# Half-tile weight buffers, a longer lead for the casts, and a third seven-product group per feed-forward block

## The chip, the cores and the metric

The kernel runs on one core of a Trainium2 chip. The metric is the device time of one execution in microseconds (us). The engines named below are PE (TensorE; PEld is its weight load), DVE (VectorE), ACT (ScalarE), POOL (GpSimd) and SP (SyncE, whose queue issues most DMAs). Each engine takes its instructions in order.

## What is computed

A trunk of two layers over 256 tokens of width 1024, float32. Cut to what matters here:

```python
D_MODEL, SEQ, DEPTH, D_FF = 1024, 256, 2, 2816

def swiglu(h, w_gate, w_up, w_down):
    return (jax.nn.silu(h @ w_gate) * (h @ w_up)) @ w_down

for l in range(DEPTH):
    x = x + 0.5 * swiglu(rms_norm(x, ffn1_norm[l]), ffn1_w_gate[l], ffn1_w_up[l], ffn1_w_down[l])
    ...            # one projection, windowed and differential attention, output projection
    x = x + 0.5 * swiglu(rms_norm(x, ffn2_norm[l]), ffn2_w_gate[l], ffn2_w_up[l], ffn2_w_down[l])
return rms_norm(x, final_norm)
```

So there are four feed-forward blocks (FFNs), two in a layer, with an attention stage ("mix") between the two of a layer. Every weight is read from HBM once or more and used on 256 tokens.

## The kernel before

**Precision.** A float32 matrix product is made of three fast ones. Each operand is split into a rounded part (`hi`, by a cast on ACT) and the rest (`lo`, by a subtraction on DVE); the product is hi·hi + lo·hi + hi·lo. Weights are split on the way in: `emit_split` (L167) casts a weight tile in pieces, each piece one ACT cast and one DVE subtraction of 128 x 1024 elements (128 x 512 for tiles in the set `fine`). So a weight tile costs ACT and DVE time as well as PE time.

**Weight tiles and their queue.** A weight tile is 512 rows by 512 columns (1 MB, held as 128 x 4 x 512), or as much in another shape. `specs` lists all tiles of the program in the order in which PE uses them. Three counters run ahead of the use: `dma` (the load, by SP, into one of N_RAW = 6 buffers `raw`), `prep` (what must be done to the raw tile first) and `split`. `weights()` (L219) hands out the next tile and first calls `ahead()` (L198), which issues whatever is due: splits up to LOOK = 2 tiles ahead of the one in use, preps one further, loads up to AHEAD = 8 tiles ahead while a raw buffer is free. The split parts lie in three whole-tile buffers `whi` and three `wlo`. In the feed-forward blocks the order in which instructions are issued is kept on every engine, so a split that is issued before a subtraction of results also runs before it.

**An FFN.** The 2816 hidden columns are taken in five groups of 512 (0 to 4) and a rest of 256. For a group, the hidden activations of 256 tokens are made from the gate and up weights; the next group's work contains the "down" product of this group's hidden values (two tiles, 24 matmuls each, L632). For it the hidden block is turned: eight PE transposes, then an ACT cast and a DVE subtraction for each of two blocks (`turn`, L618, and `split`, L485; the result is the tile `s` in the profile, called hT here). A plain group takes eight products of 12 matmuls: two token halves, two halves of the contraction, gate and up.

**By seven.** The groups in SEVEN = (2, 4) take seven products instead (Strassen's scheme, over token halves by contraction halves by gate/up; `by_seven`, L579). The sums of the token side are made once in an FFN (`make_sums`, during group 1). The sums on the weight side are made for each group by `seven` (L115) from four quarters: a (gate, upper rows), b (up, upper rows), c (up, lower rows), d (gate, lower rows). The nine steps of a seven group, in the order of use:

| step | weights | product | how the raw tile is made |
|---|---|---|---|
| 1 | a | p1 | load |
| 2 | b + c | p7 | load b, then POOL issues an accumulating DMA of c onto it (the "c-gather") |
| 3 | a + b + c | p6 | DVE adds a onto b's buffer (two adds); then POOL adds b from HBM onto a's buffer (the "b-gather") |
| 4 | down, first half | | load |
| 5 | d | p2 | load |
| 6 | a + b + c + d | p4 | DVE adds b's buffer onto d's (two adds); b's buffer is then free |
| 7 | a + b | p5 | a's buffer, after the b-gather |
| 8 | c | p3 | load |
| 9 | down, second half | | load |

hT is turned between p7 and p6; the combinations of products (u2, u3, g0, g1) are DVE instructions on 128 x 512 elements, the two `up` are the last step of the hidden values.

Loads go out on SP in the order of steps, each when a raw buffer comes free. Both gathers read 1 MB from HBM again, on POOL's DMA queue. The c-gather is issued behind its own load (`behind`, L164), the b-gather behind the two adds of step 3.

The diff touches, besides these, `tokens`, `narrow` and `prod` (which part of a tile a matmul reads), the calls of `weights` in `ffn`, `ffn_end`, `ffn_close`, `mix` and `out_part`, and the buffers of the token sums (L320).

Of the kernel before, what the change touches and what calls it, by code (L numbers as in the profile page):

```python
# [10 lines left out]
F32R = mybir.dt.float32r  # L11
AF = mybir.ActivationFunctionType
ALU = mybir.AluOpType
# [11 lines left out]
QA, KA, VA, QB, KB, VB = 0, 512, 640, 768, 1280, 1792  # L25
BIG = 1e33

LOOK, AHEAD = 2, 8
N_RAW, N_HI, N_LO = 6, 3, 3
N_S4 = 16  # L30
SEVEN = (2, 4)


@with_exitstack
def trunk(ctx: ExitStack, tc: tile.TileContext, x, n1, g1, u1, d1, nm, w_in, sink,
# [128 lines left out]
        if s.behind is not None:  # L164
            s.behind()

    def emit_split(i):  # L167
        s = specs[i]
        kn, n, raw = s.kn, s.n, raws[s.src]
        hi = wp.tile([P, kn, n], F32R, tag="whi", bufs=N_HI, name=nm_("whi"))  # L170
        lo = wp.tile([P, kn, n], F32R, tag="wlo", bufs=N_LO, name=nm_("wlo"))
        loaded[i] = (hi, lo)
        cuts = [0, kn // 2, kn] if i > 1 and (i not in fine or kn < 4) else [kn * j // 4 for j in range(5)]
        for a, b in zip(cuts, cuts[1:]):
            if n == D:
                views = [(t[0][:, a:b, c:c + 512], t[1][:, a:b, c:c + 512], t[2][:, a:b, c:c + 512])
                         for t in [(raw, hi, lo)] for c in (0, 512)]
            elif i not in paired:
                views = [(raw[:, a:b], hi[:, a:b], lo[:, a:b])]
            else:  # L180
                views = [(raw.rearrange("p k (s c d) -> p c k s d", s=2, c=2)[:, c, a:b],
                          hi.rearrange("p k (c s d) -> p c k s d", s=2, c=2)[:, c, a:b],
                          lo.rearrange("p k (c s d) -> p c k s d", s=2, c=2)[:, c, a:b]) for c in range(2)]
            for r_, h_, l_ in views:
                act.copy(h_, r_)
                dve.tensor_tensor(l_, r_, f(h_), op=ALU.subtract)
            if i < 2:
                yield
        for k in s.free:
            raws.pop(k)  # L190

    def emit_early(i):
        yield from emit_dma(i)
        yield from emit_split(i)

    at = dict(use=0, dma=2, prep=2, split=2)

    def ahead(n):  # L198

        n = min(n, len(specs) - 1)  # L200
        while True:
            if at["split"] <= n and at["prep"] > at["split"]:
                for _ in emit_split(at["split"]):
                    pass
                at["split"] += 1
            elif at["prep"] <= min(n + 1, len(specs) - 1) and at["dma"] > at["prep"] and \
                    (specs[at["prep"]].prep is None or at["split"] >= at["prep"]):
                if specs[at["prep"]].prep is not None:
                    specs[at["prep"]].prep()
                at["prep"] += 1  # L210
            elif at["dma"] < min(at["use"] + AHEAD, len(specs)) and (specs[at["dma"]].moves is None or len(raws) < N_RAW):
                if specs[at["dma"]].moves is not None:
                    for _ in emit_dma(at["dma"]):
                        pass
                at["dma"] += 1
            else:
                break

    def weights(look=LOOK):  # L219
        i = at["use"]  # L220
        at["use"] += 1
        if i > 1:
            ahead(i + look)
        return loaded.pop(i)

    for l in range(DEPTH):
        def ffn_specs(wg, wu, wd):
# [45 lines left out]
    class Norm:  # L273
# [30 lines left out]
        def make_sums(self):  # L304

            self.sm = []

            def part(b, t):

                vs = [f(self.xs[2 * b + i]) for i in range(2)]  # L310
                return [[v[:, :, c + t * P:c + (t + 1) * P] for v in vs] for c in (0, S)]

            def make(x, y, op, rest):
                v = tmp().rearrange("p a (c s) -> p (a c) s", c=2)
                for i in range(2):
                    vi = v[:, 2 * i:2 * i + 2]
                    dve.tensor_tensor(vi, x[i], y[i], op=op)
                    for z, o in rest:
                        dve.tensor_tensor(vi, vi, z[i], op=o)
                sm = blk().rearrange("p a (c s) -> p (a c) s", c=2)  # L320
                act.copy(sm[:, :, 0:P], v)
                dve.tensor_tensor(sm[:, :, P:S], v, f(sm[:, :, 0:P]), op=ALU.subtract)
                self.sm.append(sm)
                return [v[:, 0:2], v[:, 2:4]]

            add, sub = ALU.add, ALU.subtract
            (t0h, t0l), (t1h, t1l), (b0h, b0l), (b1h, b1l) = [part(b, t) for b in range(2) for t in range(2)]
            s1 = make(b1h, t1h, sub, [(b1l, add), (t1l, sub)])
            yield
            s2 = make(s1, t0h, add, [(t0l, add)])  # L330
            yield
            make(t1h, t0h, sub, [(t1l, add), (t0l, sub)])
            yield
            make(b0h, s2, sub, [(b0l, add)])
            yield
# [53 lines left out]
    def take_x(k):  # L389
# [8 lines left out]
        elif k == 1:  # L398
            for e in (g, u, g, u):
                next(e)  # L400
            norm.pair(2)
            ahead(2)
            norm.pair(3)
        elif k == 2:
            ahead(3)
            for t in range(2):
                for h in range(2):
                    norm.squares(t, h * 512, 512)
            norm.stats()
            constants()  # L410
# [60 lines left out]
            dve.tensor_scalar_mul(gsub[:, l:l + 1], gcol[:, 48 + l:49 + l], 1.0 - lam_init[l])  # L471


    def tokens(accs, xs, w, k0, ks=range(4), first=0, last=KC - 1, order=None):

        hi, lo = w
        for k, t in (order or [(k, t) for k in ks for t in range(2)]):
            kk = k0 + k
            xv = xs[kk // 2][:, kk % 2]
            xh, xl = xv[:, t * P:(t + 1) * P], xv[:, S + t * P:S + (t + 1) * P]  # L480
            pe.matmul(accs[t], lhsT=xh, rhs=hi[:, k], start=kk == first, stop=False)
            pe.matmul(accs[t], lhsT=xl, rhs=hi[:, k], start=False, stop=False)
            pe.matmul(accs[t], lhsT=xh, rhs=lo[:, k], start=False, stop=kk == (last if isinstance(last, int) else last[t]))

    def split(dst, src, scale=None):  # L485

# [7 lines left out]

    def narrow(acc, w, j, xs, kcs, first, last):

        hi, lo = w
        for i, (wk, xk) in enumerate(kcs):
            wh = hi[:, wk, j * P:(j + 1) * P]
            wl = lo[:, wk, j * P:(j + 1) * P]  # L500
            xv = xs[xk // 2][:, xk % 2]
            pe.matmul(acc, lhsT=wh, rhs=xv[:, 0:S], start=first and i == 0 and j == 0, stop=False)
            pe.matmul(acc, lhsT=wh, rhs=xv[:, S:512], start=False, stop=False)
# [43 lines left out]
    def ffn(norm, aside=None, before=None, final=False):  # L547
# [19 lines left out]
            return h  # L567

        def prod(xo, w):
            hi, lo = w  # L570
            acc = bank()
            for k in range(4):
                xh, xl = xo(k)
                pe.matmul(acc, lhsT=xh, rhs=hi[:, k], start=k == 0, stop=False)
                pe.matmul(acc, lhsT=xl, rhs=hi[:, k], start=False, stop=False)
                pe.matmul(acc, lhsT=xh, rhs=lo[:, k], start=False, stop=k == 3)
            return acc

        def by_seven(h, g):  # L579
# [8 lines left out]
            p1 = prod(norm.quarter(0, 0), weights())  # L588
            m1 = flat()
            act.copy(m1, p1)  # L590
            p7 = prod(norm.summed(2), weights())
            hT = turn(h, 2)
            p6 = prod(norm.summed(1), weights())
            u2 = put(flat(), p6, m1, ALU.subtract)
# [42 lines left out]
        if before is None:  # L637
            before = norm.late
        before(0)
        ws = (weights(), weights(LOOK - 1))  # L640
        for k in (0, 2):
            if k:
                before(1)
# [40 lines left out]
    def ffn_end(parts, last):  # L684
# [4 lines left out]
        w = {0: weights()}  # L689

        def group(h, order, a=None, c=slice(None), first=0):
            tokens(a or accs[h], hT, [t[:, :, c] for t in w[h]], G4, first=first, last=last[h], order=order)

        def tail(h, order=BY_TOKENS, a=None, c=slice(None)):
            tokens(a or accs[h], [None] * (2 * NGRP) + hE, [t[:, h, :, c] for t in w["rest"]], 4 * NGRP, last=last[h], order=order)

        group(0, [(k, t) for k in range(3) for t in range(2)])
        hE.extend(rest())
        group(0, [(3, t) for t in range(2)])
        w["rest"] = [t.rearrange("p k (h n) -> p h k n", h=2) for t in weights()]  # L700
        w[1] = weights(LOOK - 1)
        return group, tail

    def ffn_close(parts, nxt):
# [4 lines left out]
        for t in range(2):  # L709
            res.add(0, t)  # L710
        tail(1)
        ahead(at["use"] + LOOK - 1)
        group(1, [(1, t) for t in range(2)])
        for j in range(2):
            nxt.pair(j)
# [7 lines left out]
    def mix(l, norm, nxt_norm):  # L723
# [68 lines left out]
            return e  # L792


        s0, s1 = first_groups(norm, (weights(), weights(LOOK - 1)))
        kept[0] = False
        k_finish(rmul(s0), 2, [("b", 0), ("b", 1)])
        k_finish(rmul(s1), 2, [("b", 2), ("b", 3)])
# [36 lines left out]
        vB = tp.tile([P, 2, 512], F32, tag="v", bufs=1, name=nm_("v"))  # L835
        vsl = [bank() for _ in range(2)]
        for k0 in (0, 4):
            hi, lo = weights()
            for k in range(4):
                kk = k0 + k  # L840
                xv = norm.xs[kk // 2][:, kk % 2]
                for t in range(2):
                    xh, xl = xv[:, t * P:(t + 1) * P], xv[:, S + t * P:S + (t + 1) * P]
                    pe.matmul(vsl[t], lhsT=xh, rhs=hi[:, k], start=kk == 0, stop=False)
                    pe.matmul(vsl[t], lhsT=xl, rhs=hi[:, k], start=False, stop=False)
                    pe.matmul(vsl[t], lhsT=xh, rhs=lo[:, k], start=False, stop=kk == KC - 1)
            if k0 == 0:
                p_a += [soft_a(2, qA1[0]), soft_a(3, qA1[1])]
                aT.append(keys_first_b(1))
# [70 lines left out]
        res = Residual(nxt_norm, accs)  # L920

        def out_part(w, k0, h, order=None):
            tokens(accs[h], oT, [t.rearrange("p k (h n) -> p h k n", h=2)[:, h] for t in w], k0, range(2), 4, 3, order)

        w = weights()
        for h in range(2):
# [112 lines left out]
```

## Time and profile before

| | |
|---|---|
| three runs | 945.32, 945.48 and 945.58 us; median 945.48 |
| the profiled execution | 945.94 us; span 944.2 us, first to last instruction |
| mean granted TensorE clock | 0.999 |
| ACT busy | 538.1 us (57% of the span) |
| POOL busy | 40.6 us, 65 instructions |
| bytes read from HBM | 184.32 MB, 196 GB/s over the span |
| SP's loads of 1 MB, median to landing | 5.1 to 6.2 us by tensor |
| POOL's gathers of 1 MB, 16 of them | 9.1 us median to landing |
| weight subtractions on DVE, 128 x 1024 | 304, mean 1219 ns each |
| weight casts on ACT, 128 x 1024 | 304, mean 1050 ns each |
| raw-buffer adds on DVE, 128 x 1024 | 32, mean 1218 ns each |
| matmuls of 512 columns | 3342, mean 392 (with `whi`) and 390 ns (with `wlo`) each |

A mean is the time from an instruction's own start to its own end. Instructions of an engine overlap at their ends, so the cost of one in a dense row is its pitch, from start to start, which is smaller. Seen from the start of the span, group 2 of the first FFN lies at about 65 to 96 us and group 4 at about 130 to 161 us.

### The profile page before, as it was taken

Reading aid. Unit: us, or ns where it says so; the run is one execution under the profiler, and the core shown is the slowest. Engines: PE = TensorE matmul, PEld = TensorE weight load, DVE = VectorE, ACT = ScalarE, POOL = GpSimd, SP = SyncE. Lnnn points to the kernel's source line nnn. Section 1 sums busy time; section 2 is a strip of 40 time slices with the busy share of each in tenths; the row PEclk is TensorE's granted clock in tenths of the full one; section 3 lists DMA queues with packets and bytes.
Section 4 is the critical chain, followed back from the end, with each engine's and each line's share of the span. In section 5 each row is a group of like instructions: output and inputs, shape, how many; then the busy total and the mean of one; then the engine's idle time right before and its main releaser. Section 6 shows DMA issues by size and latency. Waiting matters only on the chain.

```text
span 944.2 us, 12633 instructions
## 1 busy us (share of the span) xinstructions
PE 931.5 (99%) x4844; PEld 790.4 (84%) x4844; DVE 718.6 (76%) x1086; ACT 538.1 (57%) x853; POOL 40.6 (4%) x65
## 2 busy tenths in 40 slices
PE   8999999999999999999999999999999999999997
PEld 6887888899888887888888888888999888888886
DVE  5689779579856589679557995887796667995983
ACT  6647546567735547446554564656676464564653
POOL 0400000000000000000000000000000000000001
PEclk9999999999999999999999999999999999999999
DMA  9959868655424829958557498586551447497631
GB/s 336 338 140 286 246 178 303 190 179 136 134 90 144 256 92 286 293 133 306 185 179 223 97 329 243 148 300 186 170 168 56 139 174 223 104 346 241 151 118 45
DMA packets 106669, 186.19 MB, mean 197 GB/s; under 512 B 3438, under 2 KB 31152, under 8 KB 106608
## 3 DMA queue, kind: packets, MB, share of 16 engines
q1 hardware_dynamic: 96816, 167.27, 52.0%
q0 software_dynamic: 8704, 17.07, 10.5%
q10 hardware_dynamic: 1088, 1.05, 0.3%
q8 instruction: 38, 0.62, 0.3%
q14 instruction: 23, 0.19, 0.1%
HBM read 184.32 MB, written 1.05 MB: 196 GB/s over the span
## 4 chain that ended last, share of the span: by engine, by line
PE 82%; DVE 11%; ACT 4%; issue 2%; DMA 0%; ACTq 0%; POOLq 0%; POOL 0%; DVEq 0%
PE ps L50 82%; DVE wlo L50 6%; DVE tmp L50 3%; ACT whi L50 3%; DVE s L50 1%; ACT s L50 1%; DVE raw L50 0%; DMA xk<-in_x_dram 0%; ACT tmp L50 0%; DVE xk L50 0%; ACTq L50 0%; POOLq L1034 0%; POOL rf L50 0%; DVE rf L50 0%; DVEq L50 0%
## 5 line engine op out<-in xcount | busy, mean ns | idle before, releaser
L50 PE MATMUL ps<-whi,s 128*128 128x512 f32 (+1 forms) x2252 | 699.4, 391 | 2.0 <-DVE s L50 2.0
L50 DVE TENSOR_TENSOR wlo<-raw,whi 128x1024 fp32r<-128x1024 f32 (+2 forms) x440 | 433.8, 1034 | 97.7 <-ACT whi L50 95.1
L50 PEld LDWEIGHTS ps<-whi,s 128*128 128x128 f32 x2252 | 419.7, 188 | 88.4 <-DVE s L50 3.7
L50 ACT CAST whi<-raw 128x1024 fp32r<-128x1024 f32 (+2 forms) x440 | 372.0, 902 | 177.2 <-PE ps L50 117.7
L50 PE MATMUL ps<-wlo,s 128*128 128x512 f32 (+1 forms) x1126 | 438.1, 389 | 0.0
L50 PEld LDWEIGHTS ps<-wlo,s 128*128 128x128 f32 x1126 | 211.8, 188 | 43.9 <-DVE wlo L50 0.2
L50 PE MATMUL ps<-s,whi 128*128 128x256 f32 x448 | 82.7, 286 | 0.0
L50 PEld LDWEIGHTS ps<-s,whi 128*128 128x128 f32 x448 | 70.1, 192 | 1.1
L50 ACT CAST s<-ps 128x512 fp32r<-128x512 f32 x48 | 26.0, 589 | 66.0 <-PE ps L50 66.0
L50 PE MATMUL ps<-s,wlo 128*128 128x256 f32 x224 | 63.3, 283 | 0.0
L50 DVE TENSOR_TENSOR s<-ps,s 128x512 fp32r<-128x512 f32 x48 | 31.0, 685 | 41.5 <-ACT s L50 41.5
L50 PEld LDWEIGHTS ps<-s,wlo 128*128 128x128 f32 x224 | 42.9, 192 | 0.0
L50 ACT CAST s<-tmp 128x512 fp32r<-128x512 f32 (+1 forms) x22 | 13.2, 602 | 49.1 <-DVE tmp L50 49.1
L50 PE MATMUL ps<-ident,s 128*128 128x128 f32 x304 | 39.6, 273 | 0.0
L50 PEld LDWEIGHTS ps<-ident,s 128*128 128x128 f32 x304 | 35.1, 141 | 4.7
L50 POOL DMA_DIRECT2D raw<-in_ffn_w_up_dram x16 | 20.8, 1298 | 412.9 <-ACT whi L50 120.0
L50 DVE TENSOR_TENSOR raw<-raw,raw 128x1024 f32<-128x1024 f32 x32 | 37.6, 1218 | 0.0
L50 ACT ACTIVATE s<-s,negm 128x256 f32<-128x256 f32 x64 | 31.8, 501 | 7.4 <-DVE negm L50 7.4
L50 ACT ACTIVATE tmp<-ps,r 128x512 f32<-128x512 f32 (+1 forms) x32 | 19.9, 636 | 28.0 <-PE ps L50 27.9
L50 DVE SCALAR_TENSOR_TENSOR s<-ps,hr,tmp 128x512 f32<-128x512 f32 (+1 forms) x32 | 20.8, 681 | 13.4 <-PE ps L50 6.9
L50 ACT ACTIVATE s<-ps,gcol 128x256 fp32r<-128x256 f32 x48 | 19.3, 474 | 19.7 <-PE ps L50 19.7
L50 DVE SCALAR_TENSOR_TENSOR s<-ps,gcol,s 128x256 fp32r<-128x256 f32 x48 | 20.3, 477 | 13.1 <-ACT s L50 13.0
(104 smaller groups left out, 411.2 us busy)
## 6 DMA issues: line engine op xcount, KB each, us to landing
raw<-in_ffn_w_down_dram SPq DMA_DIRECT2D x44, 1024.0 KB, 5.2
raw<-in_ffn_w_gate_dram SPq DMA_DIRECT2D x39, 1024.0 KB, 6.2
raw<-in_ffn_w_up_dram SPq DMA_DIRECT2D x39, 1024.0 KB, 5.1
raw<-in_ffn_w_up_dram POOLq DMA_DIRECT2D x16, 1024.0 KB, 9.1
raw<-in_w_in_dram SPq DMA_DIRECT2D x14, 1024.0 KB, 5.1
raw<-in_ffn_w_gate_dram SPq DMA_DIRECT2D x8, 512.0 KB, 3.8
raw<-in_ffn_w_up_dram SPq DMA_DIRECT2D x8, 512.0 KB, 5.0
raw<-in_w_in_dram SPq DMA_DIRECT2D x8, 512.0 KB, 4.5
```

The costliest lines, as they stand in the source:

```text
L50: ins = issue(*a, **k)
```

## The change

Split weights now lie in 14 buffers of half a tile (tag `w`; a half is a `hi` and a `lo` buffer, so seven halves are held) in place of three whole tiles of each kind. `ahead` counts halves: at the first use of a tile, splits are issued up to six halves further, and one more when its second half is first touched (`Split.part`). For p7, and at a few places where two tiles are used by turns, no new split is issued at the second half (`held`), and the first call issues two halves fewer (`less`). SEVEN becomes (2, 3, 4): group 3 of each FFN is made by seven products too, and the three groups follow one another. AHEAD is 10. The pool `s4` has 14 blocks instead of 16; the four token sums lie in buffers of the tags `q` and `v`, which the mix stage uses at other times. What is computed stays the same.

```diff
-LOOK, AHEAD = 2, 8
-N_RAW, N_HI, N_LO = 6, 3, 3
-N_S4 = 16
-SEVEN = (2, 4)
+AHEAD = 10
+N_RAW, N_W = 6, 14
+N_S4 = 14
+SEVEN = (2, 3, 4)
...
-    def emit_split(i):
+    class Split:
+        def __init__(self, i):
+            self.i, self.n, self.parts, self.held = i, specs[i].n, [], False
+
+        def part(self, k, c=slice(None), h=None):
+            if h is None:
+                h, k = divmod(k, 2)
+            if h and not self.held:
+                self.held = True
+                ahead(2 * self.i + 1 + HALVES)
+            return [t[:, k, c] for t in self.parts[h]]
+
+    def emit_split(i, j):
         s = specs[i]
...
+        shape = (P, 8, P) if s.n == 256 else (P, 2, 512)
+        hi, lo = [wp.tile(list(shape), F32R, tag="w", bufs=N_W, name=nm_("w")) for _ in range(2)]
+        loaded[i].parts.append((hi, lo))
...
+        m = shape[1] // 2 if i < 2 or i in fine else shape[1]
+        for a in range(0, shape[1], m):
+            r_, h_, l_ = [t[:, a:a + m] for t in (raw, hi, lo)]
+            act.copy(h_, r_)
+            dve.tensor_tensor(l_, r_, f(h_), op=ALU.subtract)
...
+    HALVES = N_W // 2 - 1
+    at = dict(use=0, dma=2, prep=2, split=4)
 
     def ahead(n):
 
-        n = min(n, len(specs) - 1)
+        n = min(n, 2 * len(specs) - 1)
         while True:
-            if at["split"] <= n and at["prep"] > at["split"]:
-                for _ in emit_split(at["split"]):
+            if at["split"] <= n and at["prep"] > at["split"] // 2:
+                for _ in emit_split(*divmod(at["split"], 2)):
                     pass
                 at["split"] += 1
-            elif at["prep"] <= min(n + 1, len(specs) - 1) and at["dma"] > at["prep"] and \
-                    (specs[at["prep"]].prep is None or at["split"] >= at["prep"]):
+            elif at["prep"] <= min(n // 2 + 1, len(specs) - 1) and at["dma"] > at["prep"] and \
+                    (specs[at["prep"]].prep is None or at["split"] >= 2 * at["prep"]):
...
-    def weights(look=LOOK):
+    def weights(less=0, held=False):
+
         i = at["use"]
         at["use"] += 1
         if i > 1:
-            ahead(i + look)
-        return loaded.pop(i)
+            ahead(2 * i + HALVES - less)
+        w = loaded[i]
+        w.held = held
+        return w
...
-                sm = blk().rearrange("p a (c s) -> p (a c) s", c=2)
+                tag, n = ("q", 3) if len(self.sm) < 3 else ("v", 1)
+                sm = tp.tile([P, 2, 512], F32R, tag=tag, bufs=n, name=nm_(tag)).rearrange("p a (c s) -> p (a c) s", c=2)
...
         def prod(xo, w):
-            hi, lo = w
             acc = bank()
             for k in range(4):
+                hi, lo = w.part(k)
                 xh, xl = xo(k)
-                pe.matmul(acc, lhsT=xh, rhs=hi[:, k], start=k == 0, stop=False)
-                pe.matmul(acc, lhsT=xl, rhs=hi[:, k], start=False, stop=False)
-                pe.matmul(acc, lhsT=xh, rhs=lo[:, k], start=False, stop=k == 3)
+                pe.matmul(acc, lhsT=xh, rhs=hi, start=k == 0, stop=False)
+                pe.matmul(acc, lhsT=xl, rhs=hi, start=False, stop=False)
+                pe.matmul(acc, lhsT=xh, rhs=lo, start=False, stop=k == 3)
             return acc
...
-            p7 = prod(norm.summed(2), weights())
+            p7 = prod(norm.summed(2), weights(2, True))
             hT = turn(h, 2)
             p6 = prod(norm.summed(1), weights())
```

The other edits pass a `Split` in place of the pair (hi, lo) to `tokens`, `narrow` and the value projection, and replace `weights(LOOK - 1)` by `weights(2)`.

More of the change, by code (lines that the diff above doesn't have):

```diff
@@ L165, in emit_dma @@
             s.behind()
-    def emit_split(i):
-        s = specs[i]
[L169 to L186, printed above, removed]
+    class Split:
[8 more added lines that the diff above has]
+            return [t[:, k, c] for t in self.parts[h]]
@@ new lines, in emit_split @@
+    def emit_split(i, j):
+        s = specs[i]
+        raw = raws[s.src]
+        if j == 0:
+            loaded[i] = Split(i)
+        shape = (P, 8, P) if s.n == 256 else (P, 2, 512)
+        hi, lo = [wp.tile(list(shape), F32R, tag="w", bufs=N_W, name=nm_("w")) for _ in range(2)]
+        loaded[i].parts.append((hi, lo))
+        if s.n == D:
+            raw = raw[:, :, j * 512:(j + 1) * 512]
+        elif i in paired:
+            raw = raw.rearrange("p k (s c d) -> p c k s d", s=2, c=2)[:, j]
+            hi, lo = [t.rearrange("p k (s d) -> p k s d", s=2) for t in (hi, lo)]
+        elif s.n == 256:
+            raw = raw[:, :, j * P:(j + 1) * P]
+        else:
+            raw = raw[:, 2 * j:2 * j + 2]
+        m = shape[1] // 2 if i < 2 or i in fine else shape[1]
[3 more added lines that the diff above has]
+            dve.tensor_tensor(l_, r_, f(h_), op=ALU.subtract)
@@ L187, in emit_split @@
             if i < 2:
                 yield
-        for k in s.free:
-            raws.pop(k)
+        if j == 1:
+            for k in s.free:
+                raws.pop(k)
     def emit_early(i):
         yield from emit_dma(i)
-        yield from emit_split(i)
-    at = dict(use=0, dma=2, prep=2, split=2)
+        for j in range(2):
+            yield from emit_split(i, j)
+    HALVES = N_W // 2 - 1
+    at = dict(use=0, dma=2, prep=2, split=4)
     def ahead(n):
-        n = min(n, len(specs) - 1)
+        n = min(n, 2 * len(specs) - 1)
@@ L401, in take_x @@
             norm.pair(2)
-            ahead(2)
+            ahead(5)
             norm.pair(3)
         elif k == 2:
-            ahead(3)
+            ahead(7)
             for t in range(2):
@@ L471, in attention_constants, with tokens @@
             dve.tensor_scalar_mul(gsub[:, l:l + 1], gcol[:, 48 + l:49 + l], 1.0 - lam_init[l])
-    def tokens(accs, xs, w, k0, ks=range(4), first=0, last=KC - 1, order=None):
-        hi, lo = w
+    def tokens(accs, xs, w, k0, ks=range(4), first=0, last=KC - 1, order=None, cols=slice(None), h=None):
         for k, t in (order or [(k, t) for k in ks for t in range(2)]):
             kk = k0 + k
+            hi, lo = w.part(k, cols, h)
             xv = xs[kk // 2][:, kk % 2]
             xh, xl = xv[:, t * P:(t + 1) * P], xv[:, S + t * P:S + (t + 1) * P]
-            pe.matmul(accs[t], lhsT=xh, rhs=hi[:, k], start=kk == first, stop=False)
-            pe.matmul(accs[t], lhsT=xl, rhs=hi[:, k], start=False, stop=False)
-            pe.matmul(accs[t], lhsT=xh, rhs=lo[:, k], start=False, stop=kk == (last if isinstance(last, int) else last[t]))
+            pe.matmul(accs[t], lhsT=xh, rhs=hi, start=kk == first, stop=False)
+            pe.matmul(accs[t], lhsT=xl, rhs=hi, start=False, stop=False)
+            pe.matmul(accs[t], lhsT=xh, rhs=lo, start=False, stop=kk == (last if isinstance(last, int) else last[t]))
     def split(dst, src, scale=None):
@@ L495, in narrow @@
     def narrow(acc, w, j, xs, kcs, first, last):
-        hi, lo = w
         for i, (wk, xk) in enumerate(kcs):
-            wh = hi[:, wk, j * P:(j + 1) * P]
-            wl = lo[:, wk, j * P:(j + 1) * P]
+            wh, wl = w.part(wk, h=j)
             xv = xs[xk // 2][:, xk % 2]
@@ L569, in prod @@
         def prod(xo, w):
-            hi, lo = w
             acc = bank()
             for k in range(4):
+                hi, lo = w.part(k)
                 xh, xl = xo(k)
-                pe.matmul(acc, lhsT=xh, rhs=hi[:, k], start=k == 0, stop=False)
-                pe.matmul(acc, lhsT=xl, rhs=hi[:, k], start=False, stop=False)
-                pe.matmul(acc, lhsT=xh, rhs=lo[:, k], start=False, stop=k == 3)
+                pe.matmul(acc, lhsT=xh, rhs=hi, start=k == 0, stop=False)
+                pe.matmul(acc, lhsT=xl, rhs=hi, start=False, stop=False)
+                pe.matmul(acc, lhsT=xh, rhs=lo, start=False, stop=k == 3)
             return acc
@@ L639, in ffn @@
         before(0)
-        ws = (weights(), weights(LOOK - 1))
+        ws = (weights(), weights(2))
         for k in (0, 2):
@@ L691, in group @@
         def group(h, order, a=None, c=slice(None), first=0):
-            tokens(a or accs[h], hT, [t[:, :, c] for t in w[h]], G4, first=first, last=last[h], order=order)
+            tokens(a or accs[h], hT, w[h], G4, first=first, last=last[h], order=order, cols=c)
         def tail(h, order=BY_TOKENS, a=None, c=slice(None)):
-            tokens(a or accs[h], [None] * (2 * NGRP) + hE, [t[:, h, :, c] for t in w["rest"]], 4 * NGRP, last=last[h], order=order)
+            tokens(a or accs[h], [None] * (2 * NGRP) + hE, w["rest"], 4 * NGRP, last=last[h], order=order, cols=c, h=h)
         group(0, [(k, t) for k in range(3) for t in range(2)])
@@ L699, in ffn_end @@
         group(0, [(3, t) for t in range(2)])
-        w["rest"] = [t.rearrange("p k (h n) -> p h k n", h=2) for t in weights()]
-        w[1] = weights(LOOK - 1)
+        w["rest"] = weights()
+        w[1] = weights(2)
         return group, tail
@@ L711, in ffn_close @@
         tail(1)
-        ahead(at["use"] + LOOK - 1)
+        ahead(2 * at["use"] - 2 + HALVES)
         group(1, [(1, t) for t in range(2)])
@@ L792, in soft_a @@
             return e
-        s0, s1 = first_groups(norm, (weights(), weights(LOOK - 1)))
+        s0, s1 = first_groups(norm, (weights(held=True), weights(2, True)))
         kept[0] = False
@@ L837, in mix @@
         for k0 in (0, 4):
-            hi, lo = weights()
+            w = weights()
             for k in range(4):
                 kk = k0 + k
+                hi, lo = w.part(k)
                 xv = norm.xs[kk // 2][:, kk % 2]
@@ L843, in mix @@
                     xh, xl = xv[:, t * P:(t + 1) * P], xv[:, S + t * P:S + (t + 1) * P]
-                    pe.matmul(vsl[t], lhsT=xh, rhs=hi[:, k], start=kk == 0, stop=False)
-                    pe.matmul(vsl[t], lhsT=xl, rhs=hi[:, k], start=False, stop=False)
-                    pe.matmul(vsl[t], lhsT=xh, rhs=lo[:, k], start=False, stop=kk == KC - 1)
+                    pe.matmul(vsl[t], lhsT=xh, rhs=hi, start=kk == 0, stop=False)
+                    pe.matmul(vsl[t], lhsT=xl, rhs=hi, start=False, stop=False)
+                    pe.matmul(vsl[t], lhsT=xh, rhs=lo, start=False, stop=kk == KC - 1)
             if k0 == 0:
@@ L922, in out_part @@
         def out_part(w, k0, h, order=None):
-            tokens(accs[h], oT, [t.rearrange("p k (h n) -> p h k n", h=2)[:, h] for t in w], k0, range(2), 4, 3, order)
+            tokens(accs[h], oT, w, k0, range(2), 4, 3, order, h=h)
         w = weights()
```

## The prediction

> **What bounds the kernel now.** I read the page's first part, then the instructions of PE in order of time, then those of DVE and SP around a seven group, then the DMA views.
>
> ```profile
> span 944.2 us, 12633 instructions
> PE 931.5 (99%) x4844; PEld 790.4 (84%) x4844; DVE 718.6 (76%) x1086; ACT 538.1 (57%) x853; POOL 40.6 (4%) x65
> ...
> PE 82%; DVE 11%; ACT 4%; issue 2%; DMA 0%; ACTq 0%; POOLq 0%; POOL 0%; DVEq 0%
> ```
>
> PE is dense, and the chain that ended last is 82% PE; DVE's 11% of it lie in the four stretches where group 1 passes into group 2. PE's timeline shows the price of a matmul and the only waits behind the start:
>
> ```profile
> 73.81 0.39 PE L50 MATMUL ps<-whi,s 128*128 128x512 f32 x1
> 74.70 0.50 PE L50 MATMUL ps<-whi,s 128*128 128x512 f32 x1 [0.51 <-DVE s L50]
> ...
> 77.10 0.39 PE L50 MATMUL ps<-wlo,s 128*128 128x512 f32 x1
> 77.33 0.62 PE L50 MATMUL ps<-whi,s 128*128 128x512 f32 x2
> 77.78 0.39 PE L50 MATMUL ps<-wlo,s 128*128 128x512 f32 x1
> ```
>
> Three matmuls from 77.10 to 77.78: 0.2267 us each. At 73.81 the next was due at 74.04 and began at 74.70, 0.66 us late, for the first hT block; that happens once in each FFN, in group 2 (four waits for DVE s).
>
> DVE in that group, in order of time (start, length, merged runs):
>
> ```profile
> 73.96 1.28 DVE L50 TENSOR_TENSOR s<-ps,s 128x512 fp32r<-128x512 f32 x2
> 75.16 2.35 DVE L50 TENSOR_TENSOR wlo<-raw,whi 128x1024 fp32r<-128x1024 f32 x2
> 77.43 2.35 DVE L50 TENSOR_TENSOR raw<-raw,raw 128x1024 f32<-128x1024 f32 x2
> 79.70 1.41 DVE L50 TENSOR_TENSOR tmp<-ps,tmp 128x512 f32<-128x512 f32 x2
> 81.02 4.62 DVE L50 TENSOR_TENSOR wlo<-raw,whi 128x1024 fp32r<-128x1024 f32 x4
> 85.56 0.68 DVE L50 TENSOR_TENSOR tmp<-ps,tmp 128x512 f32<-128x512 f32 x1
> ```
>
> No gap: DVE is full here. Pitches by starts: weight subtraction and raw add 1.135 (81.02 to 85.56 is four), u2 and u3 together 1.32, other combinations 0.60, the hT pair 1.20. SP's loads follow it:
>
> ```profile
> 74.07 6.10 SPq L159 DMA_DIRECT2D raw<-in_ffn_w_gate_dram  x2
> 83.40 2.64 SPq L159 DMA_DIRECT2D raw<-in_ffn_w_up_dram  x2
> 88.54 3.23 SPq L159 DMA_DIRECT2D raw<-in_ffn_w_down_dram  x2
> ```
>
> The first goes out as the down tile's subtractions end (73.96); the second, at 79.80, as the adds of step 6 end and free b's buffer; 83.40 and 85.67 as the halves of d and a's second product end. Loads wait for raw buffers, and six are all there are. How full the DMA engines are in the two parts of the group (PE, PEld, DVE, ACT and POOL busy, clock, DMA share, GB/s):
>
> ```profile
> 64.50:80.00 15.50, 14.99 (x70) 12.19 (x69) 15.31 (x15) 9.51 (x12) 1.28 (x1) 1.00 0.55 129
> 80.00:96.30 16.30, 16.30 (x73) 13.34 (x72) 16.27 (x19) 13.19 (x14) 0.00 (x0) 1.00 0.94 329
> ```
>
> In the second part plain loads alone take 0.94. Two gathers, at 104.60 (three loads issued within 8.2 us behind it) and at 131.08 (none for 6 us), and POOL's queue over the span:
>
> ```profile
> raw<-in_ffn_w_up_dram POOLq DMA_DIRECT2D x1, 1024.0 KB, 13.9
> ...
> raw<-in_ffn_w_up_dram POOLq DMA_DIRECT2D x1, 1024.0 KB, 8.4
> ...
> q0 software_dynamic: 8704, 17.07, 10.5%
> ```
>
> A gather beside a busy load queue lands 5.5 us later. Its own work is 10.5% of 944.2 over 16 gathers, 6.2 us; a load's is 52% over 159.5 MB-tiles, 3.1 us.
>
> **The sum** is made against the profiled execution's 945.94 us; the median shown is 0.46 lower.
>
> **1. Fewer matmuls.** Eight products become seven in group 3 of four FFNs: 4 x 12 x 0.2267 = **-10.88**.
>
> **2. The lead and the hold at p7.** Splits may run one to two halves further. DVE sat idle 3.10 us before hT in group 1 (until ACT s), where one more tile (2 x 1.135) fits. So the 0.66 wait of group 2 should go: 4 x 0.66 = **-2.64**. Bounds: 0 if the lead is never built, -2.64 else. In every order the casts needed up to the down tile stand before hT, so the hold keeps the old order there and costs nothing itself. The earliest first hT block ends 1.99 us after the turn starts (135.75 to 137.74, group 4, unhindered); PE needs it after eight transposes (0.79) and p6 (2.72). So DVE can never be more than 0.79 + 2.72 - 1.99 = 1.52 us early at hT.
>
> **3. DVE in three seven groups on end.** A cycle from hT to hT is 18 subtractions and 4 adds (22 x 1.135 = 24.97), u2 and u3 1.32, five other combinations 3.00, two `up` 1.32, hT 1.20: 31.81. PE needs 132 x 0.2267 + 0.79 = 30.72. DVE loses 1.09 at each passage from a seven group to the next. Before, a plain group (12 subtractions, DVE idle 9.5 of 33.7 us from 96.3 to 130) made that good; now 2 to 3 and 3 to 4 have no such cover.
>
> **4. The c-gather of the following group.** Its b cannot be loaded before a raw buffer is free: step 4's buffer goes to the next a, and the next one is b's own, at the end of step 6's adds. Call this t = 0. On DVE follow, before the next group's step 2: ten subtractions 11.35, u2 and u3 1.32, g0 and g1 1.20, two p5 subtractions 1.20, together 15.07; its ACT cast comes 1.15 earlier, so the data is wanted at 13.9. On the DMA side: SP 0.1, load 5.1 (rows at 83.40 and 366.67), landing to POOL's start 0.6 (386.57 to 387.13 and alike), together 5.8, then the gather's landing time G. Late by 5.8 + G - 13.9 = **G - 8.1**.
>
> G from both sides: 8.2 to 8.5 with few loads near, 13.9 in the densest row. Here SP issues, as DVE frees buffers, down at 2.4, d at 6.0, c at 8.2 and the second down at 11.1: in the gather's first 5.3 us three loads, more than in the row at 104.60 (0.7, 4.2, 8.2 behind it). In the 2.4 us behind the issue at 104.60 the DMA share was 0.39, so some 1.5 us pass before data flows; the rest of 8.4 without loads is 6.9, of 13.9 with them 12.4: the gather has about half of the engines while loads are queued. Its own 6.2 less the tail, 5.95, doubled and 1.5 in front: I take G = **13.4**, an estimate from these rows, 5.3 us late. The low end is 8.2, 0.1 us late. The high end is a gather behind all five loads: 1.5 + 5 x 3.1 + 6.2 - 5.8 + 0.6, G = 18.
>
> Behind the waiting ACT cast stand all later casts, and on DVE `up`, the adds of step 3, the b-gather and hT: nothing fills the gap, and all of it reaches PE at p7, p6 and the down tile. For each FFN: 2 x (1.09 + 5.3) - 1.52 = 11.26; four: **+45.0**.
>
> **5. Costed at nothing.** ACT's six more casts per FFN (0.98 each): ACT is 22.7 of 31.8 us busy in group 2; without that cover they would be 5.9 per FFN. The b-gather: issued 11.5 us of DVE work ahead of t = 0 and wanted 2.4 behind (1.135 x 2 + 1.32 - 1.15), 13.9 for at most 9.9 in its eight rows; if late, it adds to the same gap. SP's emission with AHEAD 10: SP waits for buffers either way. Half buffers: the same casts in the same sizes. 14 blocks in mix: if one is short, a block waits for eight transposes (1.03 us), at most 4 in all; DVE is 53.1 of 64.0 us busy there, so I take 0.
>
> Sum: 945.94 - 10.88 - 2.64 + 45.0 = 977.4, against the median **977**.
>
> [...]
>
> **Rivals.** *The gather lands in time* (the other side): place, the same wait; it decides at G = 9.5, where 932.42 (945.94 less the first two terms) + 4 x (2(G - 7.01) - 1.52) reaches the old time. For it: the gathers at 319.96 and 387.13 took 9.1 and 9.2 with two loads near. Against: 0.94 busy without it. At G = 8.4 to 9.2: 937 to 944; with no wait, only the 1.09s, 935. *Half as bad*, G 9.7 to 11.5 (rows 10.7 and 11.2): 947 to 962. *The lead is never built* (no change in what it says): no -2.64, no 1.52: 986. *Loads first*: G = 18, up to 1014.
>
> **Chances.** Forecast (G 11.5 to 14.5: 962 to 987) 0.50; gather in time 0.28; no change 0.04; half as bad 0.10; lead not built 0.04; loads first 0.04. Within 0.2%, about what a measurement of this kernel can tell, is 943.6 to 947.4. Faster 0.28, same 0.04, slower 0.68. Range 938 to 987; the likeliest case's own is 962 to 987.
>
> **What would show it.** Right: 3294 matmuls of 512 columns; HBM read up by 8.4 MB; in groups 2 and 3 of every FFN an ACT cast that waits some 5 us for DMA raw (eight in all), the gather before it landing in 13 to 14 us; then PE waits in p7, p6 and the down tile, 6 us a passage; the chain of waits passing through DMA raw. Wrong: gathers under 9.5 us; or loads of b that go out before step 6's adds end; or DVE not dense between those adds and the next step 2.

## The result, and the profile after

The changed kernel takes 989.39 us (median of 4 runs, 987.98 to 991.0) against 945.53 us (4 runs, 945.32 to 945.7): 1.0464 of the time before, 95% interval 1.0447 to 1.048. The profiled execution took 991.0 us, span 989.2. So the change made the kernel slower, by the mechanism forecast, but by 43.9 us where 31.5 were forecast; the time lies 2.4 us above the range.

The page of the changed kernel, first part, then the chain that ended last, the DMA queues, bytes read, and POOL's gathers (count, size, median to landing):

```profile
span 989.2 us, 12977 instructions
...
PE 942.1 (95%) x4796; PEld 792.8 (80%) x4796; DVE 781.8 (79%) x1130; ACT 563.4 (57%) x857; POOL 51.7 (5%) x73
...
q0 software_dynamic: 12928, 25.46, 14.7%
...
HBM read 192.71 MB, written 1.05 MB: 196 GB/s over the span
...
PE 73%; DMA 12%; DVE 10%; issue 3%; ACT 1%; POOLq 0%; ACTq 0%; POOL 0%; DVEq 0%
...
raw<-in_ffn_w_up_dram POOLq DMA_DIRECT2D x24, 1024.0 KB, 10.3
```

PE has 48 instructions fewer and reads 8.4 MB more come from HBM, as planned. The chain, which held no DMA in the middle before, is 12% DMA now. PE's idle time is 989.2 - 942.1 = 47.1 us (before 944.2 - 931.5 = 12.7). And PE is *busier*, 942.1 for 931.5, with 10.88 us less to do: its matmuls became slower in places, by 21.5 us in sum.

The chain in the second FFN, from group 2 to the turn in group 3, in order of time (start, length, what):

```profile
373.38 2.28 DVE raw L50 x2
...
375.67 5.24 DMA raw<-in_ffn_w_up_dram
...
381.47 13.73 DMA raw<-in_ffn_w_up_dram
...
395.30 1.06 ACT w L50
...
397.52 0.74 DVE s L50
398.26 1.14 DVE w L50
399.40 2.27 DVE raw L50 x2
401.67 0.60 DVE tmp L50
...
403.32 0.52 DVE s L50
```

This is part 4 of the prediction as a picture: the adds of step 6 end and free b's buffer, b loads in 5.24 us, the c-gather takes 13.73, then come the cast, an `up`, a weight subtraction, the adds of the next step 3, a combination, and the second `up`. PE and DVE at that place (start, length; in brackets the idle time before, and what ended it):

```profile
392.77 3.33 PE L50 MATMUL ps<-w,s 128*128 128x512 f32 x14
396.40 0.73 PE L50 MATMUL ps<-w,q 128*128 128x512 f32 x2 [0.30 <-ACT w L50]
397.65 3.00 PE L50 MATMUL ps<-w,q 128*128 128x512 f32 x10 [0.52 <-DVE w L50]
404.12 1.09 PE L50 MATMUL ps<-ident,s 128*128 128x128 f32 x8 [3.47 <-DVE s L50]
405.26 4.60 PE L50 MATMUL ps<-w,q 128*128 128x512 f32 x12
409.70 3.59 PE L50 MATMUL ps<-w,s 128*128 128x512 f32 x15
```

```profile
389.83 1.23 DVE L50 TENSOR_TENSOR w<-raw,w 128x1024 fp32r<-128x1024 f32 x1 [0.60 <-ACT w L50]
390.97 1.28 DVE L50 TENSOR_TENSOR tmp<-tmp,ps 128x512 f32<-128x512 f32 x2
396.38 1.22 DVE L50 TENSOR_TENSOR w<-raw,w 128x1024 fp32r<-128x1024 f32 x1 [4.13 <-ACT w L50]
```

PE waits 0.30 and 0.52 us in p7, then 3.47 us in one piece in front of the eight transposes of the turn. Behind that wait, p6's twelve matmuls take 4.44 us, from 405.26 to the start of the down tile's at 409.70, where 2.72 are normal. The stretches around it, cut where the granted clock changes (length, then PE, PEld, DVE, ACT and POOL busy with instructions, clock, DMA share, GB/s), say why:

```profile
398.74:402.15 3.41, 1.76 (x7) 0.81 (x5) 3.41 (x4) 1.42 (x2) 0.00 (x0) 1.00 0.00 0
402.15:405.56 3.41, 1.39 (x9) 1.15 (x10) 3.41 (x5) 3.41 (x5) 1.28 (x1) 1.00 0.38 54
405.56:408.98 3.42, 3.42 (x9) 2.65 (x8) 3.42 (x5) 2.50 (x4) 0.00 (x0) 0.50 1.13 206
408.98:412.39 3.41, 3.41 (x16) 2.79 (x15) 3.41 (x4) 0.23 (x1) 0.00 (x0) 1.00 1.04 346
```

The granted clock is 0.50 from 405.56 to 408.98, and in group 4's passage from 439.70 to 446.52. In the 3.41 us ahead of the first of these PE was idle for 2.02, in the 3.41 us ahead of the second for 1.74. The forecast had no such term.

### The profile page after: what moved, and what is told of

Same layout as the page of the kernel before. It is cut to its first block, busy times and chain, and to the rows that moved or that the text cites. A ratio compares the mean times of both kernels' runs of the same rounds, so it can differ in the third digit from the quotient of the medians.

```text
span 989.2 us, 12977 instructions
## 1 busy us (share of the span) xinstructions
PE 942.1 (95%) x4796; PEld 792.8 (80%) x4796; DVE 781.8 (79%) x1130; ACT 563.4 (57%) x857; POOL 51.7 (5%) x73
## 4 chain that ended last, share of the span: by engine, by line
PE 73%; DMA 12%; DVE 10%; issue 3%; ACT 1%; POOLq 0%; ACTq 0%; POOL 0%; DVEq 0%
PE ps L50 73%; DMA raw<-in_ffn_w_up_dram 11%; DVE w L50 4%; DVE raw L50 3%; DVE s L50 2%; ACT w L50 1%; DMA xk<-in_x_dram 1%; DVE tmp L50 0%; DVE distA L50 0%; ACTq L50 0%; ACT tmp L50 0%; DVE distB L50 0%; DVE xk L50 0%; POOLq L1057 0%; POOL rf L50 0%
## 5 line engine op out<-in xcount | busy, mean ns | idle before, releaser
L50 PE MATMUL ps<-w,s 128*128 128x512 f32 (+1 forms) x2754 | 635.8, 390 | 0.0
L50 PEld LDWEIGHTS ps<-w,s 128*128 128x128 f32 x2754 | 512.9, 188 | 104.7
L50 DVE TENSOR_TENSOR w<-raw,w 128x1024 fp32r<-128x1024 f32 (+1 forms) x440 | 467.5, 1095 | 114.5 <-ACT w L50 111.9
L50 ACT CAST w<-raw 128x1024 fp32r<-128x1024 f32 (+1 forms) x440 | 395.9, 947 | 210.6 <-PE ps L50 93.5
L50 PE MATMUL ps<-w,q 128*128 128x512 f32 x432 | 121.9, 432 | 8.2 <-ACT tmp L50 4.1
L50 PEld LDWEIGHTS ps<-w,q 128*128 128x128 f32 x432 | 88.3, 210 | 34.2 <-DVE w L50 8.7
L50 PE MATMUL ps<-s,w 128*128 128x256 f32 x672 | 84.1, 285 | 0.0
L50 PEld LDWEIGHTS ps<-s,w 128*128 128x128 f32 x672 | 81.7, 192 | 1.1
L50 PE MATMUL ps<-w,v 128*128 128x512 f32 x144 | 34.6, 389 | 0.0
L50 DVE TENSOR_TENSOR tmp<-ps,tmp 128x512 f32<-128x512 f32 x48 | 33.0, 687 | 0.4
```

Source lines behind the costliest of these rows:

```text
L50: ins = issue(*a, **k)
```

## The experiments

**Is it the passage from one seven group to the next?** Two kernels with two seven groups each, and so with the same number of matmuls as the kernel before: apart, and side by side.

```diff
-SEVEN = (2, 3, 4)
+SEVEN = (2, 4)
```

> The changed kernel with SEVEN = (2, 4) again: half-tile buffers, the lead, the hold at p7 and the 14 blocks stay. My theory (the loss lies where one seven group follows another): no ACT cast waits long for DMA raw, the granted clock is back at 0.999, and the time is that of the kernel before less the four waits of 0.66 us, 943 us (941 to 945.5). Rival (the new buffers or the order of casts cost the time): over 960 us.

Measured: 942.02 us (941.66 to 943.33), 0.9965 of the kernel before (0.9952 to 0.9977).

```diff
-SEVEN = (2, 3, 4)
+SEVEN = (2, 3)
```

> SEVEN = (2, 3): as many matmuls as with (2, 4), but one passage from a seven group to the next in each FFN. My theory: each passage costs some 5.4 us of PE waiting and some 2.2 us of half clock behind it, and in the first FFN 4.3 us more for the attention constants that now stand in the passage: 943 + 4 x 7.6 + 4.3 = 978 us (965 to 985). Rival (it is the third seven group, DVE and DMA work as such, that costs, not the adjacency): within 3 us of the run with (2, 4).

Measured: 978.37 us, 1.0346 (1.033 to 1.0362). The waits of PE and ACT in the two, apart first (us in total, times, longest):

```profile
ACT w L50 <- DMA raw<-in_ffn_w_up_dram: 2.6, 3, 1.8
...
PE ps L50 <- ACT tmp L50: 0.3, 1, 0.3
```

```profile
ACT w L50 <- DMA raw<-in_ffn_w_up_dram: 18.8, 5, 5.8
PE ps L50 <- DVE s L50: 13.9, 4, 3.5
PE ps L50 <- ACT tmp L50: 4.9, 2, 4.2
```

The new buffers, the lead and the hold are no loss; by themselves they are a gain of 3.5 us, the old waits for hT being gone. Four passages, one of them with the attention constants in it, cost 36.4 us, with as many matmuls.

**Is the late c-gather the cause, or is DVE the limit anyway?** The loads of b and a change places: b takes the raw buffer that the down tile frees, 5.7 us earlier.

```diff
-        return [Step(4, 512, load(a), key=a, free=[]),
-                Step(4, 512, load(b), key=b, behind=gather(c, b), free=[]),
+        return [Step(4, 512, load(b), key=b, src=a, behind=gather(c, b), free=[]),
+                Step(4, 512, load(a), key=a, src=b, free=[]),
```

> Only the order of two loads is turned: b of the next group takes the raw buffer that the down tile frees, a takes the one that b frees; the c-gather then starts 5.7 us earlier. My theory (the late c-gather is the cause): its wait of some 5 us goes, PE's waits fall under 2 us each, the clock stays near 1.0, and the time is 936 to 944 us (1.09 us of DVE per passage, and the constants in the first FFN, stay). Rival (DVE is the limit in three seven groups on end, whatever the gather does, or the DMA engines are full): over 960 us.

Measured: 955.4 us (951.45 to 956.52), 1.0096 (1.0074 to 1.0118): 34 us less than the changed kernel, and between the two theories, above the 936 to 944 of the one and below the 960 of the other. At seven of the eight passages the gather still takes 12.1 to 13.4 us (15.0 at the eighth), it only starts in time; the long ACT waits for it are gone (1.3 us at most in a passage). What is left is on DVE:

```profile
374.92 1.21 DVE L50 TENSOR_TENSOR w<-raw,w 128x1024 fp32r<-128x1024 f32 x1
376.74 1.23 DVE L50 TENSOR_TENSOR w<-raw,w 128x1024 fp32r<-128x1024 f32 x1 [0.60 <-ACT w L50]
...
378.48 1.21 DVE L50 TENSOR_TENSOR w<-raw,w 128x1024 fp32r<-128x1024 f32 x1
380.30 1.23 DVE L50 TENSOR_TENSOR w<-raw,w 128x1024 fp32r<-128x1024 f32 x1 [0.60 <-ACT w L50]
...
397.11 2.35 DVE L50 TENSOR_TENSOR raw<-raw,raw 128x1024 f32<-128x1024 f32 x2
...
430.44 2.35 DVE L50 TENSOR_TENSOR raw<-raw,raw 128x1024 f32<-128x1024 f32 x2
```

From the adds of one group to those of the next are 33.33 us, not 31.81. Twice in a group DVE waits 0.60 us for the cast of a tile's second half. In ACT's order a silu stands between the casts of the two halves, and it waits for DVE's g0 or g1 first. Whole-tile casts had no such place; in the changed kernel these waits lay in the shadow of the gather.

**The two silu behind the product** (on top of b first):

```diff
             w = weights()
-            silu(g0, g0, 0)
             p4 = prod(norm.quarter(1, 1), w)
+            silu(g0, g0, 0)
...
-            silu(g1, g1, 1)
             p5 = prod(norm.summed(0), w)
+            silu(g1, g1, 1)
```

> The run with b loaded first, and the two silu of a seven group on ACT issued behind the product that follows, so that they no longer stand between the casts of a tile's two halves. My theory (half-tile casts put a silu between them, DVE then waits 0.60 us twice in a group, and with the gather out of the way these waits are on the path): the cycle of a seven group falls from 33.3 to 32.1 us, the time by up to 9.6 us to 946 us (944 to 950). Rival (the 0.60 waits are idle time that costs nothing): 953 to 957 us.

Measured: 945.34 us (942.74 to 947.27), 0.9994 (0.9983 to 1.0004); 10.1 us less than with b first alone.

**The attention constants.** In the first FFN, `aside` is called at the head of group 3, which is now in the passage. It is moved behind group 4, in the changed kernel and in the improved one:

```diff
-            if n == 3 and aside is not None:
-                aside()
...
+        if aside is not None:
+            aside()
         gu = [bank(), bank()]
```

> The changed kernel with one edit: the attention constants of the first FFN (one PE transpose, some 3.9 us of DVE and ACT work with its wait) are made behind group 4 instead of at the head of group 3. My theory (they stand in the passage from group 2 to 3, where nothing covers them): that passage falls by about 4 us, 985 us (983 to 987). Rival (they fill DVE time that is idle anyway): 988 to 991 us.

Measured: 985.92 us (985.26 to 986.7), 3.5 us less than the changed kernel. PE's time from the turn in group 3 to the turn in group 4 of the first FFN falls from 41.71 to 37.01 us.

> The run before it, with the attention constants moved behind group 4 as well. My theory: about 4 us less than that run, 941 to 943 us (938 to 945), three seven groups no slower than the kernel before, and near the 942.0 us of the two-group kernel; what is left is 1.09 to 1.4 us of DVE per passage. Rival (a third seven group can't pay because DVE is full): 945.5 us or more.

Measured: 940.76 us (939.6 to 942.06), 0.995 of the kernel before (0.9938 to 0.9963). DVE and PE in it:

```profile
388.35 2.36 DVE L50 TENSOR_TENSOR raw<-raw,raw 128x1024 f32<-128x1024 f32 x2
...
399.52 2.35 DVE L50 TENSOR_TENSOR w<-raw,w 128x1024 fp32r<-128x1024 f32 x2
...
420.31 2.37 DVE L50 TENSOR_TENSOR raw<-raw,raw 128x1024 f32<-128x1024 f32 x2
```

```profile
PE ps L50 <- DVE s L50: 5.0, 4, 2.2
```

The cycle is 31.96 us here, 31.95 to 32.08 at six of the eight passages, and DVE runs its two halves without a gap. PE waits for DVE four times, 5.0 us in all. Two of these waits, 1.65 and 2.18 us, lie at the other two passages, from group 3 to 4 in the third and fourth FFN, where the cycle is 33.02 and 33.57 us: there the c-gather is late again. In the fourth FFN ACT waits 3.13 us for it, and DVE then for ACT:

```profile
867.50 2.00 ACT L50 CAST w<-raw 128x1024 fp32r<-128x1024 f32 x2 [3.13 <-DMA raw<-in_ffn_w_up_dram]
868.58 1.23 DVE L50 TENSOR_TENSOR w<-raw,w 128x1024 fp32r<-128x1024 f32 x1 [1.51 <-ACT w L50]
```

This version, with three seven groups, is 0.5% faster than the kernel before. Against the two-group kernel (942.02) its intervals overlap, so these runs do not show that the third seven group, with 10.88 us less work for PE, gains anything.

**Is the half clock a cost of its own?** In groups 3 and 4 of every FFN p7 is computed twice, the second time into the bank that the turn then overwrites: 96 matmuls more. The eight waits that they fill are 3.45 to 3.48 us each, but for one of 2.48 in the first FFN.

```diff
-            p7 = prod(norm.summed(2), weights(2, True))
-            hT = turn(h, 2)
+            w7 = weights(2, True)
+            p7 = prod(norm.summed(2), w7)
...
+            hT = turn(h, 2, again if g - 1 in SEVEN else None)
```

> In groups 3 and 4 the twelve matmuls of p7 are computed a second time, into the PSUM bank that the turn then overwrites, so 96 matmuls (21.8 us) are added in the eight waits of 3.47 us ahead of the turn. My theory (a wait of 3.47 us lowers the granted clock, and the slow matmuls behind the last passage of each FFN cost 1.7 to 2.7 us): the wait falls to some 0.8 us, the clock stays at 1.0, and the kernel gets faster by 6 to 10 us, to 979 to 984 us, although it does more. Rival (the matmuls behind the wait are slow for another reason, such as late operands): 988 to 995 us.

Measured: 984.08 us (983.91 to 985.68), 1.0411 (1.0395 to 1.0426): 5.3 us less than the changed kernel, with 21.8 us more work for PE. The mean granted clock went from 0.974 to 0.995. In the second FFN, third group:

```profile
402.02 1.09 PE L50 MATMUL ps<-ident,s 128*128 128x128 f32 x8 [0.76 <-DVE s L50]
```

The gain is a little under the low end. One reason is that the clock still fell: it is 0.98 in the mean from 100 to 200 us and from 400 to 500 us, and 0.76 in the stretch from 436 to 440 us, behind waits of 1.64 and 0.53 us.

**The hold at p7** taken out of the improved kernel:

```diff
-            p7 = prod(norm.summed(2), weights(2, True))
+            p7 = prod(norm.summed(2), weights())
```

> The run with b first, silu later and the constants moved, without the hold at p7: two more half-tile subtractions (2.27 us) stand on DVE ahead of hT. My theory (DVE is at most 1.5 us early at hT): PE waits 0.8 to 2.3 us longer for hT in the three seven groups of each FFN, 10 to 25 us more. Rival (the lead covers it, the hold does nothing): within 2 us of the run with the hold.

Measured: 964.57 us (961.47 to 967.16), 23.8 us more than with the hold. PE waits in front of the down tile in group 2 and 3, in the second FFN:

```profile
365.22 12.55 PE L50 MATMUL ps<-w,s 128*128 128x512 f32 x47 [3.22 <-DVE s L50]
399.01 10.96 PE L50 MATMUL ps<-w,s 128*128 128x512 f32 x47 [1.07 <-DVE s L50]
```

The 3.22 us are more than the 0.8 to 2.3 expected: in group 2 not only two subtractions but also the two adds of step 6 (from 362.21) now run on DVE ahead of hT (364.48). So the longer lead needs the hold; without it the lead costs more than it gives.

## Why the prediction was right in kind and wrong in size

*Matmuls (-10.88) and the lead (-2.64):* right. PE lost 48 instructions, and with two seven groups apart 942.02 was measured where 945.53 - 2.64 gives 942.9. That DVE would come to hT as early as it can, 1.52 us, was not right: in group 2 of the second FFN the first hT block ends at 370.51, and PE, whose turn starts at 367.84, is through p6 at 367.84 + 0.79 + 2.72 = 371.35, so DVE is 0.84 us early; the other FFNs give the same.

*DVE's 1.09 us a passage:* nearly right where nothing else stands in the way, 31.96 against 30.72 in the last version, so 1.24. That it is gap-free with half-tile casts was wrong (33.33 with the silu between the halves), and it was one of the prediction's own signs of being wrong; in the changed kernel this lay under the gather.

*The late c-gather:* right. G was taken as 13.4; the eight gathers at the passages took 13.3, 12.7, 13.7, 13.6, 13.6, 13.7, 13.4 and 13.1. Adds to adds is 37.33 us on average without the first FFN's first passage (forecast 31.81 + 5.3 = 37.1). The forecast's rivals all fall: the gather was not in time, the lead was built, the loads did not go first. That G itself came out so close is partly luck. It was put together as 1.5 us before data flows and the rest at half of the engines; the 0.25 us left out as its tail was the author's estimate. The gather issued at 381.47 moves nothing for its first 4.8 us, while SP's loads (queue q1) have the engines, and then has two thirds of them (packets, MB, share of the 16 engines):

```profile
q1 hardware_dynamic: 705, 1.41, 91.9%
...
q0 software_dynamic: 527, 1.05, 66.6%
q1 hardware_dynamic: 654, 1.28, 42.6%
```

The first line is the whole traffic from 381.47 to 386.2, the other two that from 386.2 to 394.7. The gather issued at 402.20, with no load near, moves its first data after 2.0 us.

*The step that failed* is the last paragraph of part 4, "all of it reaches PE at p7, p6 and the down tile", and with it the 11.26 per FFN. PE's time from turn to turn, less 30.72, and what p6 lost behind the last turn (from the start of the turn to the first matmul of the down tile, less the 3.62 of group 2):

| us | FFN 1 | 2 | 3 | 4 | forecast for each |
|---|---|---|---|---|---|
| group 2 to 3 | 5.78 | 5.56 | 5.43 | 5.10 | 4.87 |
| group 3 to 4 | 10.99 | 6.70 | 6.46 | 6.17 | 6.39 |
| behind the last turn | 1.88 | 2.40 | 1.67 | 2.71 | 0 |

The sum is 60.9 where 45.0 were forecast. The wait gathers in one place: the second `up` stands on DVE behind the first half of the next step 3, the turn needs its result, so PE stands still for 3.47 us before it ever comes to p6. Behind that wait the granted clock is 0.50, from 405.56 to 408.98. Ahead of group 4 the slow matmuls lie inside the time that DVE needs anyway; behind the last turn no wait is left to hide them, which makes 8.7 us of the table. That they are hidden ahead of group 4 is read from the table's second row, 6.44 us in the mean of the last three FFNs where 6.39 were forecast. The twice computed p7 shows the half clock as a cost of its own (-5.3 net). The second missing term is the constants of the first FFN: the forecast does not name them, part 5 included, and they add some 4.5 us there (10.99 against 6.44 in the mean of the others); moving them took that passage to 6.29 and gave 3.5 us in all. The third is 1.52 - 0.84 = 0.68 us per FFN at hT. Together they make 8.7 + 4.5 + 4 x 0.68 = 15.9, and the table stands 15.9 above the forecast. The whole sum with the table, 945.94 - 13.52 + 60.9 = 993.3, is 2.3 us above the profiled 991.0. About 1.0 us of that is in the 30.72: with two seven groups apart, a passage from turn to turn in which nothing waits took 30.84 us (352.42 to 383.26), and the table has eight of them. Where the other 1.3 us lie stays open.

What stands ahead of a fall of the clock can be read from the traces. In the changed kernel's, between the first 12 us and PE's last matmul, the points at which it changes lie whole multiples of 3.413 us apart, and its stretches at half last 3.41, 6.82 or, once, 13.65 us. In the run with b first, waits of 1.97, 1.96 and 2.00 us in front of the turn were followed by half, half and full clock: p6's twelve matmuls behind them took 4.18, 4.56 and 3.04 us. Cut at such points, the first two waits lie in one stretch each, the third lies across a point. The first and the third, with the 3.41 us behind each:

```profile
420.69:424.11 3.42, 1.46 (x9) 0.96 (x8) 3.42 (x5) 3.34 (x4) 1.28 (x1) 1.00 0.13 23
424.11:427.52 3.41, 3.41 (x13) 2.92 (x12) 3.41 (x4) 3.31 (x6) 0.00 (x0) 0.50 1.07 178
...
888.32:891.73 3.41, 1.75 (x8) 1.13 (x6) 3.41 (x5) 3.05 (x4) 1.28 (x1) 1.00 0.09 33
891.73:895.14 3.41, 3.02 (x16) 2.47 (x17) 3.41 (x4) 3.41 (x6) 0.00 (x0) 1.00 0.93 141
```

PE is idle for 1.96 us in the first stretch and for 1.66 in the third. In the changed kernel's trace, between the first 12 us and PE's last matmul, the clock was halved behind eight full-clock stretches, and PE was idle for 1.74 to 3.31 of the 3.41 us in them; in all others it was idle for 1.64 or less. In the run without the hold two waits of nearly the same length went differently: behind 3.22 us the clock was 0.55 from 365.2 to 369 us and 47 matmuls took 12.55 us, behind 3.27 us (548.05 to 551.31) 47 matmuls took 10.95. Counted on from the half-clock stretch at 365.2 us, a point falls between 549.5 and 549.9, an estimate from these numbers, so the second wait lay across a point. No run moved a wait across a point by intent, so this is a reading of the traces and not a test.

## What to carry to other kernels

A step that spares the busiest engine 2.7 us must be paid for on the others: compare, for the new steady state alone, each engine's work and each loop "buffer free, load, second transfer, cast" with the time that the busy engine leaves. When a transfer is late, look first at which buffer it had to wait for: exchanging two loads gave back 34 of 44 us. And ask where a wait will come to lie, not only how long it is: a wait of 3.47 us was followed by 3.41 us at half clock, and 96 useless matmuls in the place of eight such waits made the kernel 5.3 us faster.

## What the runs showed of the hardware

In the changed kernel's trace, between the first 12 us and PE's last matmul, the granted clock changed only at points whole multiples of 3.413 us apart. It went to half eight times, PE having been idle for 1.74 to 3.31 of the 3.41 us ahead, and stayed there for 3.41 to 13.65 us. At or behind each of the seven waits of 3.45 to 3.48 us in front of the turn it was 0.50; of three waits of about 2 us with b first, two were followed by p6's twelve matmuls in 4.18 and 4.56 us and one by the same in 3.04.

In the changed kernel an accumulating 1 MB transfer from POOL's queue took 8.2 to 9.1 us when no load was issued in the 5 us behind it, and 12.7 to 13.7 us at the eight passages, with three loads issued from 1.0 us before it to 6.4 us behind it. The first data moved 2.0 us behind the issue in the one case and 3.2 to 5.2 us in the other. In the kernel before, its 16 transfers took 8.2 to 13.9 us.
